# A hybrid decoder trunk on one core: all four FFNs begin with two eight-product pairs, with the token scales between them

## The chip, the cores and the metric

The kernel runs on one core of one Trainium2 chip. Its engines are TensorE (PE, with its weight loads as PEld), VectorE (DVE), ScalarE (ACT), GpSimd (POOL) and SyncE (SP); SP and POOL issue most of the DMAs. The metric is device time in microseconds (us) of one execution; lower is better.

## The reference, cut to what matters

Two layers over 512 tokens of width 1024, all in float32. Each layer has two half-step SwiGLU FFNs (width 2816) around a token mixer (retention in layer 0, forgetting attention in layer 1), and then a gated per-layer embedding ("ple"). So the order is FFN 0, retention, FFN 1, ple 0, FFN 2, attention, FFN 3, ple 1, final norm.

```python
def rmsnorm(x, w):
    y = xf * lax.rsqrt(jnp.mean(xf * xf, axis=-1, keepdims=True) + EPS)
    return (y * w).astype(x.dtype)

def swiglu(x, w_in, w_out):
    g, u = jnp.split(x @ w_in, 2, axis=-1)
    return (jax.nn.silu(g) * u) @ w_out
...
        h = h + 0.5 * swiglu(rmsnorm(h, nw[0]), ffn_w_in[i, 0], ffn_w_out[i, 0])
        hn = rmsnorm(h, nw[1])
        h = h + retention(hn, ...)   # layer 1: forgetting_attention
        h = h + 0.5 * swiglu(rmsnorm(h, nw[2]), ffn_w_in[i, 1], ffn_w_out[i, 1])
        gate = jax.nn.sigmoid(rmsnorm(h, nw[3]) @ ple_w_gate[i])
        h = h + gate * (p[i] @ ple_w_proj[i])
```

## The kernel before, in words

The residual stream `h` lies transposed in SBUF: 8 blocks of 128 features x 512 tokens. Every operand of a product is split into a high and a low fp32r half, and a product is three matmuls (high x high, high x low, low x high). A row norm is not applied to the operands beforehand: only the gain is, and the products are multiplied by the token's scale afterwards. The scale comes in two steps. `Norm.columns` sums the squares over the features with eight small matmuls (L310 in `over_tokens`) and takes the reciprocal root on ScalarE and VectorE (L448 to L452, tile `cols`). `Norm.rows` spreads it over the partitions with four transposes (L443, `spread`) and a ScalarE copy (L437, tile `rows`). The square sum `acc` is split into halves by `halved` (L287, L288, tile `tmp`) when its last block is in.

An FFN's input weights come as 22 `Pair`s, each one gate tile and one up tile of 128 outputs. A pair is taken in one of two ways:

- **Eight products** (`plain`, L507): the plain block products, 96 matmuls of 128x128 by 256 tokens. The pair's two parts `q` and `r` (512 KB each) stand in the plan as ordinary chunks, each cast by ScalarE (L78) and subtracted on VectorE (L79).
- **Seven products** (`one`, `two`, `three`, L476): a Winograd form over 2 x 2 blocks, 84 matmuls. It needs sums of the weight's quarters (`emit_sums`: four additions L140, four casts L78 and four subtractions L79, tiles `sums` and `s`), one quarter negated (tile `a`: L116, L117 and an accumulating DMA on POOL's queue, L118), and of the operand also sums of quarters (`quarters`, L360 to L396). `first` loads `q` and splits it, either on ScalarE and VectorE (`direct`) or, otherwise, through another accumulating DMA on POOL's queue. `two` copies a bank (L525), adds (L526), copies again (L528) and adds (L529); `finish` adds on (L542 to L544) and calls `gated`, which multiplies by `rows`, applies Silu and splits the result (L549 to L554, L287, L288).

`PLAIN` says how many pairs of each FFN take eight products: (2, 0, 2, 2). `CHUNKS` cuts the 22 pairs into three chunks; behind each chunk `out_blocks` multiplies its results by the output weights (L296 to L298, 128x512) and adds them to `h` (L568, L571), in the last chunk with the next norm's `block`.

The order on TensorE is the order of the Python code. The queues of the other engines are laid out by a planner that goes by the order in which instructions are traced, by dependences and by its own estimate of when each is ready; on the chip each queue is then worked off in order. Weights follow a written plan, `W.plan`, in which an eight-product pair stands as the two entries `q` and `r` and a seven-product pair as one `Pair`: `take` makes sure that `LOOKAHEAD` = 2 entries behind the one taken have been emitted, and `emit` calls `emit_sums` after each. `W.open` (called ahead of the stage that precedes the FFN's own code) sets from when an FFN's sums may be emitted; in the kernel before, sums of the two pairs next to be used are allowed at once. There are four raw buffers (`wraw`) and three split buffers (`w`) for weights.

How each FFN begins, in TensorE's order:

- FFN 0: `plain(0)`, `plain(1)`, `one(2)`, columns, `two(2)`, `one(3)`, rows, then `gated(0)`, `gated(1)` on the other engines, `two(3)`.
- FFN 1: `one(0)`, `one(1)`, `two(0)`, `two(1)`, columns, `three(0)`, rows.
- FFN 2 and 3: `plain(0)`, columns, `plain(1)`, `one(2)`, rows, `gated(0)`, `gated(1)`, `two(2)`.

`norms[4].extra` and `norms[6].extra` make the norms ahead of FFN 2 and 3 also split the second half of the even blocks (form `b12`), which the eight products need and the seven don't; FFN 0's norm does this in `Norm.plain`.

Of the kernel before, what the change touches and what calls it, by code (L numbers as in the profile page):

```python
# [13 lines left out]
AF = mybir.ActivationFunctionType  # L14
ALU = mybir.AluOpType
# [13 lines left out]
KEPT = 7  # L29
PLAIN = (2, 0, 2, 2)  # L30
CHUNKS = [((0, 6), (6, 14), (14, 22)) if n else ((0, 8), (8, 16), (16, 22)) for n in PLAIN]
H2 = S // 2
# [3 lines left out]
class Pair:  # L36
# [3 lines left out]
    def __init__(self, ffn, q, r):  # L40
        self.ffn, self.q, self.r, self.direct = ffn, q, r, False
# [13 lines left out]
class Weights:  # L55

    def __init__(self, nc, raw_pool, pool):
        self.nc, self.raw_pool, self.pool = nc, raw_pool, pool  # L60
        self.plan, self.ready, self.used = [], [], 0
        self.low = nc.vector
        self.limit, self.spare = None, []
        self.sum_pool, self.open_ffn, self.pairs_used = None, None, 0

    def emit(self, upto):
# [63 lines left out]
    def emit_sums(self):  # L130

        nc = self.nc
        pairs = [p for p in self.plan[: len(self.ready)] if isinstance(p, Pair) and p.ffn == self.open_ffn]
        for pair in pairs[: self.pairs_used + 2]:
            if hasattr(pair, "s"):
# [19 lines left out]
    def open(self, ffn, pool):  # L155
        self.open_ffn, self.sum_pool, self.pairs_used = ffn, pool, 0
        self.emit_sums()

    def take(self, src):
# [13 lines left out]
def trunk(ctx, tc, a):  # L173
    nc = tc.nc
# [14 lines left out]

    W = Weights(nc, wraw, wpool)  # L190

# [125 lines left out]
    class Norm:  # L317
# [107 lines left out]
        def columns(self):  # L425

            total = over_tokens(self.acc_parts)
            self.c = stat.tile([P, NT], F32, name="cols")
            self.v = stat.tile([P, NT], F32, name="cv")
            t = stat.tile([P, NT], F32, name="ct")  # L430
            mean_eps(self.v, total)
            rsqrt(self.c, self.v, t)

# [12 lines left out]
    def rsqrt(out, v, t):  # L446

        nc.scalar.activation(t, v, AF.Sqrt)  # L448
        nc.vector.reciprocal(out, t)
        nc.vector.tensor_tensor(out=t, in0=out, in1=out, op=ALU.mult)  # L450
        nc.vector.scalar_tensor_tensor(out=t, in0=t, scalar=-0.5, in1=v, op0=ALU.mult, op1=ALU.mult)
        nc.vector.scalar_tensor_tensor(out=out, in0=t, scalar=1.5, in1=out, op0=ALU.add, op1=ALU.mult)  # L452

# [32 lines left out]
    def ffn(i, n, nxt, stack, apool, meanwhile=None):  # L486
# [87 lines left out]

        if PLAIN[i]:
            done = PLAIN[i]
            whole = [plain(m) for m in range(done - 1)]
            if i:
                n.columns()
            whole.append(plain(done - 1))  # L580
            start(done)
            one(done)
            if not i:
                n.columns()
                two(done)
                start(done + 1)
                one(done + 1)
            n.rows()
            for m, (g, u) in enumerate(whole):
                gated(m, g, u, True)  # L590
            two(done + 1 if not i else done)
            begun = done + (1 if i else 2)
        else:
            for m in (0, 1):
                start(m)
                one(m)
            two(0)
            two(1)
            n.columns()
            three(0)  # L600
            n.rows()
            finish(0)
            begun, done = 2, 1
        for c, (k0, k1) in enumerate(chunks):
# [564 lines left out]
    norms = [Norm(nw(i), *where[i]) for i in range(8)] + [Norm(fw)]  # L1169
    norms[4].extra = norms[6].extra = ua  # L1170
    first = W.emit_parts(((0, 1), (1, 2), (2, 4)))
    next(first)
# [134 lines left out]
```

## Time and profile before

| | |
|---|---|
| median of the runs shown | 2255.05 us (2253.7 to 2256.75, 3 runs) |
| the profiled execution's own time | 2254.57 us |
| its span | 2252.8 us |
| TensorE busy | 2158.8 us, 96% of the span |
| VectorE, ScalarE, POOL busy | 1467.5, 1211.5, 436.7 us |
| granted TensorE clock, mean | 0.983 of full |
| HBM traffic | 117 GB/s over the span |

The profile is of one execution. In a timeline row stand start and duration in us, engine, line, operation, tiles (out<-in), shape and count, and in brackets the engine's idle time ahead of it with what ended it. In a window row, busy time of each engine stands with the number of instructions, and PEclk is the share of its full clock that TensorE was granted. Matmuls overlap in TensorE's pipeline, so that one of 256 columns is shown as some 276 ns long while in an unbroken run they start 115 ns apart.

### The profile page before, as it was taken

What the parts mean: (1) busy time and instruction counts of PE and PEld (TensorE: products, weight loads), DVE (VectorE), ACT (ScalarE), POOL (GpSimd) and SP (SyncE); (2) the same over time, 40 slices, a digit from 0 to 9 for tenths busy, and PEclk for the clock granted to TensorE, in tenths of its full rate; (3) what the DMA queues carried; (4) which work ended last, traced back from release to release, by engine and by line L of the source; (5) the groups of instructions that cost most, each with busy time, mean ns of one, the idle gap of its engine ahead of it and who ended that gap; (6) DMA issues with size and microseconds to landing.
All of it is one profiled execution on the core that took longest, in us unless ns stands there. A gap on an engine that the chain in (4) does not pass through costs nothing.

```text
span 2252.8 us, 34423 instructions
## 1 busy us (share of the span) xinstructions
PE 2158.8 (96%) x13501; PEld 1940.0 (86%) x13501; DVE 1467.5 (65%) x2661; ACT 1211.5 (54%) x2050; POOL 436.7 (19%) x326
## 2 busy tenths in 40 slices
PE   7999999999999899999997999999899999999998
PEld 7899997888888698988976999898778798999987
DVE  8686766353442876766758677775764686877764
ACT  7465553333233664554545656464786775554553
POOL 0010003444444010110110001013333200110144
PEclk9999999999999999999998999999999999999999
DMA  5465462222222354654522456463222234655531
GB/s 179 104 164 150 137 159 94 88 90 84 86 84 75 108 144 128 154 137 122 133 97 85 113 150 164 129 166 94 88 81 76 75 105 116 166 146 143 150 103 38
DMA packets 84882, 264.98 MB, mean 118 GB/s; under 512 B 9312, under 2 KB 12896, under 8 KB 84720
## 3 DMA queue, kind: packets, MB, share of 16 engines
q1 hardware_dynamic: 63328, 209.78, 28.2%
q0 software_dynamic: 20160, 51.91, 13.8%
q8 instruction: 106, 1.74, 0.3%
q10 hardware_dynamic: 1232, 1.09, 0.2%
q14 instruction: 56, 0.46, 0.1%
HBM read 260.62 MB, written 2.13 MB: 117 GB/s over the span
## 4 chain that ended last, share of the span: by engine, by line
PE 78%; DVE 8%; ACT 6%; issue 3%; DMA 3%; POOL 1%; SPq 0%; DVEq 0%; ACTq 0%; POOLq 0%
PE bank L476 30%; PE bank L298 13%; PE bank L296 13%; PE bank L297 13%; DMA wraw<-in_ffn_w_in 3%; PE bank L507 2%; PE bank L679 2%; PE bank L680 2%; PE bank L681 2%; DVE w L79 1%; DVE sums L140 1%; ACT p L982 1%; ACT w L78 1%; POOL w L79 1%; ACT p L984 1%
## 5 line engine op out<-in xcount | busy, mean ns | idle before, releaser
L78 ACT CAST w<-wraw 128x1024 fp32r<-128x1024 f32 (+1 forms) x245 | 248.6, 1022 | 456.0 <-PE bank L298 276.0
L298 PE MATMUL bank<-unit_a,w 128*128 128x512 f32 x736 | 287.4, 391 | 4.8 <-DVE w L79 3.1
L296 PE MATMUL bank<-unit_a,w 128*128 128x512 f32 x736 | 288.8, 392 | 2.1 <-ACT w L78 2.1
L78 ACT CAST s<-sums 128x512 fp32r<-128x512 f32 x328 | 197.7, 617 | 166.2 <-DVE sums L140 113.8
L297 PE MATMUL bank<-unit_a,w 128*128 128x512 f32 x736 | 286.9, 390 | 0.2 <-DVE unit_a L288 0.2
L79 DVE TENSOR_TENSOR s<-sums,s 128x512 fp32r<-128x512 f32 x328 | 220.4, 685 | 90.6 <-ACT s L78 90.1
L298 PE MATMUL bank<-unit_d,w 128*128 128x512 f32 (+1 forms) x712 | 270.2, 380 | 6.4 <-DVE w L79 6.4
L296 PE MATMUL bank<-unit_d,w 128*128 128x512 f32 (+1 forms) x712 | 271.2, 381 | 2.8 <-ACT w L78 1.8
L79 POOL TENSOR_TENSOR w<-wraw,w 128x1024 fp32r<-128x1024 f32 x90 | 217.0, 2414 | 287.2 <-ACT w L78 275.3
L297 PE MATMUL bank<-unit_d,w 128*128 128x512 f32 (+1 forms) x712 | 270.2, 379 | 1.8 <-DVE unit_d L288 1.8
L79 DVE TENSOR_TENSOR w<-wraw,w 128x1024 fp32r<-128x1024 f32 (+1 forms) x155 | 179.5, 1164 | 40.2 <-ACT w L78 40.0
L118 POOL DMA_DIRECT2D a<-in_ffn_w_in x82 | 71.8, 876 | 684.9 <-ACT a L117 531.8
L476 PE MATMUL bank<-unit_b,s 128*128 128x256 f32 x904 | 191.3, 278 | 0.0
L476 PE MATMUL bank<-unit_a,s 128*128 128x256 f32 x1314 | 188.4, 281 | 2.0 <-ACT unit_a L360 1.0
L476 PE MATMUL bank<-unit_d,s 128*128 128x256 f32 x1140 | 179.0, 277 | 0.0
L476 PEld LDWEIGHTS bank<-unit_a,s 128*128 128x128 f32 x1314 | 169.8, 192 | 3.0 <-ACT unit_a L360 1.2
L568 DVE SCALAR_TENSOR_TENSOR tmp<-bank,rows 128x512 f32<-128x512 f32 x96 | 66.0, 689 | 162.8 <-PE bank L298 161.5
L298 PEld LDWEIGHTS bank<-unit_a,w 128*128 128x128 f32 x736 | 138.2, 188 | 36.1 <-DVE w L79 5.3
L296 PEld LDWEIGHTS bank<-unit_a,w 128*128 128x128 f32 x736 | 138.3, 188 | 32.8 <-ACT w L78 4.5
L298 PEld LDWEIGHTS bank<-unit_d,w 128*128 128x128 f32 x712 | 136.0, 191 | 32.6 <-DVE w L79 8.3
L297 PEld LDWEIGHTS bank<-unit_a,w 128*128 128x128 f32 x736 | 138.3, 188 | 28.3 <-DVE unit_a L288 0.5
L296 PEld LDWEIGHTS bank<-unit_d,w 128*128 128x128 f32 x712 | 136.3, 191 | 30.2 <-ACT w L78 3.4
(266 smaller groups left out, 4754.4 us busy)
## 6 DMA issues: line engine op xcount, KB each, us to landing
wraw<-in_ffn_w_in SPq DMA_DIRECT2D x174, 512.0 KB, 4.2
wraw<-in_ffn_w_out SPq DMA_DIRECT2D x64, 512.0 KB, 5.1
w<-in_ffn_w_in POOLq DMA_DIRECT2D x58, 512.0 KB, 5.5
a<-in_ffn_w_in POOLq DMA_DIRECT2D x82, 256.0 KB, 6.2
wraw<-in_ffn_w_out SPq DMA_DIRECT2D x32, 384.0 KB, 3.8
wraw<-in_ret_qk SPq DMA_DIRECT2D x16, 512.0 KB, 3.5
wraw<-in_ret_v SPq DMA_DIRECT2D x16, 512.0 KB, 3.6
wraw<-in_ret_g SPq DMA_DIRECT2D x16, 512.0 KB, 3.5
```

Of the source, the lines that this page charges most:

```text
L78: self.nc.scalar.copy(hi, raw)
L79: self.low.tensor_tensor(out=lo, in0=raw, in1=hi.bitcast(F32), op=ALU.subtract)
L118: self.nc.gpsimd.dma_start(out=lo, in_=src, accum_op=ALU.add)
L296: nc.tensor.matmul(out, wh, xh, start=first, stop=False)
L297: nc.tensor.matmul(out, wh, xl, start=False, stop=False)
L298: nc.tensor.matmul(out, wl, xh, start=False, stop=last)
L476: add = lambda w, x, start, stop: nc.tensor.matmul(out, w, x, start=start, stop=stop, skip_group_check=True)
L507: nc.tensor.matmul(o[:, HALVES[t]], x[:, ks], y, start=k == t == q == 0, stop=k == KB - 1 and q == 2, skip_group_check=True,)
L568: nc.vector.scalar_tensor_tensor(out=t1, in0=o, scalar=-0.5, in1=n.r, op0=ALU.mult, op1=ALU.mult)
L679: nc.tensor.matmul(os[t], xh, wh[:, js], start=k == 0, stop=False)
L680: nc.tensor.matmul(os[t], xh, wl[:, js], start=False, stop=False)
L681: nc.tensor.matmul(os[t], xl, wh[:, js], start=False, stop=k == KB - 1)
```

## The change

All four FFNs get `PLAIN` = 2 and the chunks (0, 6), (6, 14), (14, 22). All four begin alike: `plain(0)`, columns, `plain(1)`, rows, `one(2)`, `gated(0)`, `gated(1)`, `two(2)`. The norm ahead of FFN 1 gets `extra = ud`. Opening an FFN no longer allows sums; `W.begin`, called right behind `n.columns()`, allows two pairs ahead, and hands over the scale's ScalarE root and its last VectorE instruction, so that sums which `begin` itself emits are queued behind these (`tc.issue_after`).

```diff
-PLAIN = (2, 0, 2, 2)
-CHUNKS = [((0, 6), (6, 14), (14, 22)) if n else ((0, 8), (8, 16), (16, 22)) for n in PLAIN]
+PLAIN = (2, 2, 2, 2)
+CHUNKS = [((0, 6), (6, 14), (14, 22)) for n in PLAIN]
...
+        self.ahead, self.behind = 0, ()
...
     def emit_sums(self):
+        with ExitStack() as order:
+            for ins in self.behind:
+                order.enter_context(self.tc.issue_after(ins.ins))
+            self.emit_sums_now()
+
+    def emit_sums_now(self):
         nc = self.nc
         pairs = [p for p in self.plan[: len(self.ready)] if isinstance(p, Pair) and p.ffn == self.open_ffn]
-        for pair in pairs[: self.pairs_used + 2]:
+        for pair in pairs[: self.pairs_used + self.ahead]:
...
     def open(self, ffn, pool):
-        self.open_ffn, self.sum_pool, self.pairs_used = ffn, pool, 0
+        self.open_ffn, self.sum_pool, self.pairs_used, self.ahead, self.behind = ffn, pool, 0, 0, ()
+
+    def begin(self, behind):
+        self.ahead, self.behind = 2, behind
         self.emit_sums()
+        self.behind = ()
...
-            rsqrt(self.c, self.v, t)
+            return rsqrt(self.c, self.v, t)
...
-        nc.scalar.activation(t, v, AF.Sqrt)
+        root = nc.scalar.activation(t, v, AF.Sqrt)
...
-        nc.vector.scalar_tensor_tensor(out=out, in0=t, scalar=1.5, in1=out, op0=ALU.add, op1=ALU.mult)
+        last = nc.vector.scalar_tensor_tensor(out=out, in0=t, scalar=1.5, in1=out, op0=ALU.add, op1=ALU.mult)
+        return root, last
...
-        if PLAIN[i]:
-            done = PLAIN[i]
-            whole = [plain(m) for m in range(done - 1)]
-            if i:
-                n.columns()
-            whole.append(plain(done - 1))
-            start(done)
-            one(done)
-            if not i:
-                n.columns()
-                two(done)
-                start(done + 1)
-                one(done + 1)
-            n.rows()
-            for m, (g, u) in enumerate(whole):
-                gated(m, g, u, True)
-            two(done + 1 if not i else done)
-            begun = done + (1 if i else 2)
-        else:
-            for m in (0, 1):
-                start(m)
-                one(m)
-            two(0)
-            two(1)
-            n.columns()
-            three(0)
-            n.rows()
-            finish(0)
-            begun, done = 2, 1
+        done = PLAIN[i]
+        whole = [plain(m) for m in range(done - 1)]
+        W.begin(n.columns())
+        whole.append(plain(done - 1))
+        n.rows()
+        start(done)
+        one(done)
+        for m, (g, u) in enumerate(whole):
+            gated(m, g, u, True)
+        two(done)
+        begun = done + 1
...
     norms[4].extra = norms[6].extra = ua
+    norms[2].extra = ud
```

More of the change, by code (lines that the diff above doesn't have):

```diff
@@ L55, with __init__ @@
 class Weights:
-    def __init__(self, nc, raw_pool, pool):
-        self.nc, self.raw_pool, self.pool = nc, raw_pool, pool
+    def __init__(self, tc, raw_pool, pool):
+        self.tc, self.nc, self.raw_pool, self.pool = tc, tc.nc, raw_pool, pool
         self.plan, self.ready, self.used = [], [], 0
-        self.low = nc.vector
+        self.low = self.nc.vector
         self.limit, self.spare = None, []
         self.sum_pool, self.open_ffn, self.pairs_used = None, None, 0
+        self.ahead, self.behind = 0, ()
     def emit(self, upto):
@@ L188, in trunk @@
     dram = ctx.enter_context(tc.tile_pool(name="dram", bufs=1, space=bass.MemoryType.DRAM))
-    W = Weights(nc, wraw, wpool)
+    W = Weights(tc, wraw, wpool)
     def unit(pool):
```

## The prediction, made before the changed kernel was built or run

> **What bounds the kernel now.** I read the page first, then TensorE stage by stage, then its waits, then the timeline around each FFN's start.
>
> ```profile
> span 2252.8 us, 34423 instructions
> PE 2158.8 (96%) x13501; PEld 1940.0 (86%) x13501; DVE 1467.5 (65%) x2661; ACT 1211.5 (54%) x2050; POOL 436.7 (19%) x326
> ```
>
> TensorE sets the time: 96% busy. But its busy share hides slow stretches, so the next view cuts the FFNs' input products (L507 eight-product pairs, L476 seven-product pairs) into windows. Columns: stretch, length, busy time of each engine, granted clock, DMA.
>
> ```profile
> core 0: us, PE busy (x) PEld busy (x) DVE busy (x) ACT busy (x) POOL busy (x), PEclk, DMA share, GB/s
> 5.59:33.32 27.73, 25.50 (x194) 24.14 (x192) 26.75 (x54) 22.82 (x42) 1.92 (x2) 1.00 0.69 220
> 33.32:94.18 60.86, 49.25 (x387) 47.87 (x385) 45.83 (x89) 39.72 (x68) 5.23 (x6) 0.92 0.49 130
> ...
> 779.99:875.09 95.10, 85.46 (x715) 84.38 (x715) 73.27 (x138) 65.93 (x113) 12.21 (x14) 0.96 0.65 159
> 920.37:1005.72 85.35, 80.79 (x674) 80.39 (x672) 63.22 (x112) 54.55 (x95) 11.37 (x13) 0.96 0.66 164
> 1051.02:1104.94 53.92, 53.92 (x470) 53.91 (x468) 40.85 (x72) 34.62 (x60) 6.11 (x7) 1.00 0.58 144
> ...
> 1240.04:1285.44 45.40, 43.63 (x379) 43.43 (x377) 35.24 (x61) 33.10 (x56) 5.24 (x6) 1.00 0.58 140
> 1827.52:1852.39 24.87, 24.18 (x201) 23.97 (x200) 21.69 (x41) 14.60 (x25) 1.76 (x2) 1.00 0.52 148
> 1852.39:1899.46 47.07, 45.30 (x378) 45.10 (x377) 35.33 (x61) 33.49 (x56) 5.23 (x6) 0.96 0.56 135
> 1933.62:2011.05 77.43, 77.43 (x674) 77.43 (x672) 63.97 (x115) 56.05 (x97) 11.37 (x13) 1.00 0.73 180
> 2056.36:2129.63 73.27, 73.27 (x638) 73.27 (x636) 55.83 (x99) 49.37 (x86) 9.61 (x11) 1.00 0.66 165
> ```
>
> The last four rows are FFN 3: two eight-product pairs (24.87), the rest of chunk 0 (47.07), chunks 1 and 2. At full pace 672 products take 77.43, 0.1152 each. FFN 1, which begins without eight-product pairs, is the next three rows above FFN 2's 45.40: 708, 672 and 468 products in 95.10 + 85.35 + 53.92 = 234.4, where 1848 x 0.1152 = 212.9: 21.5 lost. FFN 0 is the first two rows: its 372 products of chunk 0 take 60.86 where FFN 2 needs 45.40.
>
> ```profile
> PE bank L476 <- ACT tmp L528: 11.1, 7, 3.2
> PE bank L443 <- DVE cols L452: 10.0, 2, 6.8
> ...
> PE bank L476 <- ACT unit_a L368: 4.5, 1, 4.5
> ...
> PE bank L476 <- DMA w<-in_ffn_w_in: 2.8, 1, 2.8
> ```
>
> These waits (total, times, longest) are those starts: the token scales (L452) hold TensorE twice, 6.8 in FFN 0 and 3.2 in FFN 1; L368 is FFN 1's first operand.
>
> ```profile
> 22.32 0.69 DVE L288 TENSOR_TENSOR tmp<-acc,tmp 128x512 fp32r<-128x512 f32 x1
> ...
> 43.06 1.29 DVE L140 TENSOR_TENSOR sums<-wraw 128x512 f32<-128x512 f32 x2
> ...
> 50.07 0.15 DVE L452 SCALAR_TENSOR_TENSOR cols<-ct,cols 128x4 f32<-128x4 f32 x1
> 50.37 1.09 PE L443 MATMUL bank<-ident,cols 128*128 128x128 f32 x4 [6.82 <-DVE cols L452]
> ```
>
> In FFN 0 the scales' last step ends at 50.2, behind sums (L140) of pairs that TensorE doesn't need yet.
>
> **Part by part.**
>
> *FFN 1, two eight-product pairs and chunks 6, 8, 8.* Products: 2 x 96 - 2 x 84 = 24 more, and each of the 192 at the pace of this row:
>
> ```profile
> 1827.68 11.51 PE bank L507 x96
> ```
>
> 0.120 each, so 192 x 0.120 + 1680 x 0.1152 = 216.5 against 212.9: +3.6 at full pace, on the path. The output products are as many, only divided otherwise: 0. Other engines, for pairs 0 and 1:
>
> ```profile
> L79 DVE TENSOR_TENSOR s<-sums,s 128x512 fp32r<-128x512 f32 x328 | 220.4, 685 | 90.6 <-ACT s L78 90.1
> L78 ACT CAST s<-sums 128x512 fp32r<-128x512 f32 x328 | 197.7, 617 | 166.2 <-DVE sums L140 113.8
> L79 DVE TENSOR_TENSOR w<-wraw,w 128x1024 fp32r<-128x1024 f32 x123 | 149.3, 1219 | 38.9 <-ACT w L78 38.8
> ```
>
> Gone from VectorE are eight additions and eight subtractions (16 x 0.685 = 11.0) and two conversions (2 x 1.22); four wide conversions come (4 x 1.22 = 4.9), and four half-width splits of `extra`, each under 0.69. VectorE has at least 5.8 less; ScalarE loses eight casts (4.9), gains two wide ones and the four splits. On POOL two accumulating DMAs fall away. SP keeps four 512 KB loads. The forms: `extra` takes four `ud` units, free when the last retention product that reads them is done, before block 7's splits.
>
> What FFN 1 will then cost I take from FFN 3, which has that form already, follows the same output helper, and shows the stalls left over: 24.87 + 47.07 + 77.43 + 73.27 = 222.6. Gain 234.4 - 222.6 = 11.8. Unknown is FFN 1's own start wait: between 0 more than FFN 3 and the 4.46 of the row below. Less is queued on VectorE now, so I take 1. **-10.8**.
>
> ```profile
> 784.45 1.18 PE L476 MATMUL bank<-unit_a,w 128*128 128x256 f32 x2 [4.46 <-ACT unit_a L368]
> ```
>
> *FFN 0: scales between the pairs.* The column sums need both halves of the squares, ready at 23.0 (L288 above), while plain pair 0 ends at 20.45. TensorE idles 2.6, sums columns to 23.9, then does pair 1 in 11.5: 35.4 instead of 33.32, +2.1. The step issues no DMA, passes nothing on SP's or POOL's queues, and keeps its two table loads on ScalarE. The idle time may cost clock too. Granted clock after pauses of 4.46, 2.8, 3.2 and, in FFN 3, 1.77 (its 47.07 less 45.30 busy):
>
> ```profile
> 780.00:788.50 8.50, 4.03 (x17) 3.74 (x18) 7.70 (x17) 6.66 (x11) 0.87 (x1) 0.62 0.72 191
> 65.70:72.50 6.80, 3.97 (x20) 3.97 (x21) 4.03 (x8) 1.50 (x4) 0.87 (x1) 0.75 0.89 233
> 800.91:806.00 5.09, 1.89 (x17) 1.89 (x17) 3.62 (x11) 3.28 (x7) 0.87 (x1) 1.00 0.93 204
> 1861.37:1867.00 5.63, 3.86 (x21) 3.87 (x22) 3.86 (x8) 4.07 (x7) 0.00 (x0) 0.74 0.24 86
> ```
>
> FFN 2's 1.77 left it at 1.00 (its row above). So of four short pauses two lowered the clock, for 6.80 x 0.25 = 1.7 and 5.63 x 0.26 = 1.5. I count half of 1.6: +0.8, bounds 0 and 1.7. [...]
>
> Then scales and the 372 products as in FFN 2: 45.40. But VectorE is full here:
>
> ```profile
> 20.45:33.32 12.87, 11.51 (x94) 11.31 (x94) 12.81 (x26) 12.39 (x24) 1.92 (x2) 1.00 0.47 116
> 33.32:43.55 10.23, 8.95 (x70) 8.14 (x68) 10.23 (x22) 9.40 (x16) 0.87 (x1) 1.00 0.47 125
> ```
>
> It forms the operands' quarters and the sums of pairs 2 and 3 at once. Ahead of pair 3's sums now come the scales (five of about 0.16) and the two gatings (six of 0.69): 4.9. In exchange the sums of pairs 4 and 5 drop behind, and there is no second pair to be begun early. The backlog costs 0 to 4.9; as VectorE has no slack I take 4.0. Chunk 0 ends at 35.4 + 0.8 + 45.4 + 4.0 = 85.6 instead of 94.18: **-8.6**.
>
> *FFN 2 and 3: scales before the first seven-product pair.*
>
> ```profile
> 1226.68 0.95 PE L310 MATMUL bank<-ones_r,tmp 128*128 128x2 f32 x8
> 1229.71 0.16 DVE L452 SCALAR_TENSOR_TENSOR cols<-ct,cols 128x4 f32<-128x4 f32 x1
> 1242.85 0.60 PE L443 MATMUL bank<-ident,cols 128*128 128x128 f32 x4
> 1250.36 0.37 ACT L528 COPY tmp<-bank 128x256 f32<-128x256 f32 x1 [0.35 <-DVE bank L526]
> 1250.79 0.50 PE L476 MATMUL bank<-unit_b,w 128*128 128x256 f32 x2 [1.77 <-ACT tmp L528]
> ```
>
> The scales are there 13 us before L443, so spreading them 24 products (2.8) earlier makes no wait. Gating starts 2.8 earlier; the pause of 1.77 (FFN 3 has the same, with the clock loss above) is ScalarE getting to L528 late, behind gating. It can go whole or not at all, if ScalarE merely does other work first. I take half, 0.9, in FFNs 1, 2 and 3: **-2.7** (bounds 0 and 3 x 1.77 + 1.5 = 6.8).
>
> *Sums behind the scales.* `take` keeps two plan entries ahead. After `plain(0)` has taken two, four entries are ready, and these are the four plain chunks, no `Pair`. So `begin` finds nothing to order and clears `behind`: the edges are never drawn, price 0. In FFN 0 and 1 sums are traced later than before all the same; in FFN 2 and 3 they stand where they stood.
>
> Sum: -10.8 - 8.6 - 2.7 = -22.1. The profiled execution took 2254.57, 0.5 under the median of 2255.05: 2254.6 - 22.1 = **2232.5**.
>
> **Rivals.**
> 1. *FFN 1's long chunk keeps its stalls.* Its chunk 1 has eight seven-product pairs before and after, and lost 85.35 - 77.43 = 7.9 in mid-course, where the chain went through weights:
>
> ```profile
> 849.52 4.74 DMA wraw<-in_ffn_w_in
> ...
> 855.71 1.05 ACT w L116
> ```
>
> A raw buffer is freed, loaded in 4.7, summed, and only then ScalarE proceeds: a ring. Against it: FFN 3's same chunk stalls nowhere. 2232.5 + 7.9 = 2240.
> 2. *FFN 0's scales stay late.* If ready sums still run first on VectorE, TensorE waits at the transposes again, 6.8 and the clock: 2232.5 + 8.3 = 2241. For it: full VectorE. Against: FFN 2's five scale steps took 3 us from L310.
> 3. *The edges are drawn after all.* Then FFN 2's early sums leave the stretch before its first pair, where TensorE starves. Of the sums tile alone:
>
> ```profile
> 1196.63:1217.00 20.37, 5.46 (x9) 0.71 0.31 91
> ```
>
> 2232.5 - 5.5 = 2227. The code speaks against it.
> 4. *Slower.* The ring of rival 1 sets the pace of every start, FFN 0's too (its 2.8 wait on a DMA), so that the order of scales is beside the point. FFN 1 then keeps its 21.5 and pays 3.6 for the 24 products, FFN 0 pays 2.1 for columns and gains nothing: 2254.6 + 5.7 = 2260. It decides once less than 5.7 of those losses go. Against it: FFN 2 and 3 have the ring and no such losses.
>
> **How the numbers follow.** Forecast (about 2223 to 2238) 0.56; rival 1 0.17; rival 2 0.11; rival 3 0.04; rival 4 0.07; something that leaves the time within 0.2% 0.05 (4.5 us: about what a measurement here can tell from no change). Faster 0.56 + 0.17 + 0.11 + 0.04 = 0.88, same 0.05, slower 0.07. Low end: no backlog, no start wait, all pauses gone: -11.8 - 13.4 - 6.8 = -32, 2222. High end: rivals 1 and 2 together, 2232.5 + 16.2 = 2249.
>
> **What would show it.** FFN 1: 192 L507 products in about 25, then 372 in 45 to 47, then 77.4 and 73.3. FFN 0: a pause near 2.6 before L310, L443 without a wait near 35.5, chunk 0 over at 83 to 88. FFN 2 and 3: L443 before L476, the 1.77 shorter, early sums (x9) where they were. Wrong would be: L476 waiting on L528 in FFN 1's chunk 1, L443 waiting on L452, or a long wait for unit_d or unit_c forms in FFN 1.

## The result and the profile after

The changed kernel took 2240.94 us (median of four runs, 2237.4 to 2245.6), the kernel before 2255.9 on the same chip (2253.7 to 2257.95): ratio 0.9935, 95% interval 0.9914 to 0.9956. It is faster, by 15 us where 22 were forecast; 2240.94 lies inside the range (2222 to 2249) and 8.4 above the predicted 2232.5.

The profiled execution was the longest of the four, 2245.6. The same program on another chip gave 0.9969 (0.9956 to 0.9982), a gain of some 6 us there. Single runs of one kernel lie 6 to 14 us apart (the retention stage alone takes 451.8, 453.4 or 455.0 in different runs of kernels with the same code there), so below I read stretches of TensorE, and compare totals only by their intervals.

The lines of the changed kernel are some 12 higher: eight-product pairs L520 (before L507), seven-product pairs L489 (L476), column sums L322 (L310), transposes of the scales L455 (L443), last step of the scales L464 (L452), the additions of `two` L538, L539, L541, L542 (L525 to L529), gating L562 to L567 (L549 to L554); a weight's cast and subtraction L79, L80 (L78, L79), its additions L148 (L140), ScalarE's write ahead of an accumulating DMA L118 (L117), and that DMA on POOL's queue L119 (L118); `split` of anything else L299, L300 (L287, L288), the operand's quarters L372, L373 (L360, L361). These are the page's first lines after:

```profile
span 2243.8 us, 34408 instructions
PE 2161.2 (96%) x13525; PEld 1942.3 (87%) x13525; DVE 1461.6 (65%) x2645; ACT 1205.9 (54%) x2036; POOL 435.2 (19%) x322
```

VectorE is 5.9 less busy, ScalarE 5.6, and TensorE has the 24 products more: the bookkeeping of the change came out as written. Next the windows after, cut as before: FFN 0's eight-product pairs and the rest of its chunk 0; the same two and chunks 1 and 2 of FFN 1; the rest of chunk 0 of FFN 2 and of FFN 3; chunk 1 of FFN 3.

```profile
core 0: us, PE busy (x) PEld busy (x) DVE busy (x) ACT busy (x) POOL busy (x), PEclk, DMA share, GB/s
5.46:38.50 33.04, 29.12 (x205) 27.65 (x204) 29.77 (x65) 25.11 (x46) 1.92 (x2) 0.90 0.64 200
38.50:92.40 53.90, 46.49 (x376) 45.50 (x374) 44.12 (x78) 37.48 (x65) 5.24 (x6) 0.94 0.55 139
777.59:802.82 25.23, 24.53 (x206) 24.32 (x204) 19.39 (x35) 13.85 (x22) 1.76 (x2) 1.00 0.51 146
802.82:849.96 47.14, 44.87 (x375) 44.67 (x373) 35.46 (x61) 33.15 (x56) 5.24 (x6) 0.96 0.57 135
884.12:962.48 78.36, 77.69 (x673) 77.49 (x672) 61.89 (x112) 54.19 (x94) 11.35 (x13) 1.00 0.70 172
1007.77:1081.04 73.27, 73.27 (x637) 73.27 (x636) 56.24 (x99) 49.65 (x86) 9.63 (x11) 1.00 0.65 163
1228.28:1273.70 45.42, 43.19 (x375) 43.00 (x373) 35.17 (x61) 32.90 (x56) 5.24 (x6) 1.00 0.58 140
1840.58:1887.95 47.37, 44.98 (x376) 44.78 (x373) 35.53 (x61) 33.24 (x56) 5.24 (x6) 0.96 0.56 134
1922.11:2001.17 79.06, 77.78 (x673) 77.57 (x672) 64.45 (x115) 55.30 (x96) 11.41 (x13) 1.00 0.70 177
```

FFN 1 now takes 25.23 + 47.14 + 78.36 + 73.27 = 224.0 instead of 234.4. FFN 0's chunk 0 ends at 92.40 instead of 94.18. FFN 2 and FFN 3 are no shorter, and FFN 3's chunk 1 is 1.6 longer. The waits of TensorE after (total, times, longest) say what stands there now:

```profile
PE bank L489 <- ACT tmp L541: 13.4, 6, 5.5
...
PE bank L322 <- ACT tmp L299: 2.2, 1, 2.2
```

The waits for the scales (10.0 in the view before) and for FFN 1's first operand (4.5) are gone. In their place stands one group that was 11.1 and is 13.4: TensorE ahead of pair 2's second half (`three`) waiting for ScalarE's second bank copy of `two` (four times at pair 2, twice more, for 0.7 and 0.3, in later chunks). FFN 2 and attention together are 0.9 longer.

### The profile page after: what moved, and what is told of

Its sections match the earlier page's. It is cut to its first block, busy times and chain, and to the rows that moved or that the text cites. A ratio compares the mean times of both kernels' runs of the same rounds, so it can differ in the third digit from the quotient of the medians.

```text
span 2243.8 us, 34408 instructions
## 1 busy us (share of the span) xinstructions
PE 2161.2 (96%) x13525; PEld 1942.3 (87%) x13525; DVE 1461.6 (65%) x2645; ACT 1205.9 (54%) x2036; POOL 435.2 (19%) x322
## 3 DMA queue, kind: packets, MB, share of 16 engines
q0 software_dynamic: 19584, 50.34, 13.5%
## 4 chain that ended last, share of the span: by engine, by line
PE 82%; DVE 8%; ACT 5%; issue 2%; DMA 1%; POOL 0%; SPq 0%; DVEq 0%; ACTq 0%; POOLq 0%
PE bank L489 30%; PE bank L310 14%; PE bank L308 14%; PE bank L309 14%; PE bank L520 4%; PE bank L674 2%; PE bank L675 2%; PE bank L676 2%; DVE w L80 1%; DMA wraw<-in_ffn_w_in 1%; DVE s L80 1%; ACT w L79 1%; ACT p L977 1%; DVE sums L148 1%; ACT p L979 1%
## 5 line engine op out<-in xcount | busy, mean ns | idle before, releaser
L79 ACT CAST w<-wraw 128x1024 fp32r<-128x1024 f32 (+1 forms) x249 | 252.9, 1023 | 465.7 <-PE bank L310 270.2
L310 PE MATMUL bank<-unit_a,w 128*128 128x512 f32 x736 | 287.9, 391 | 4.8 <-DVE w L80 3.1
L310 PE MATMUL bank<-unit_d,w 128*128 128x512 f32 (+1 forms) x712 | 269.9, 379 | 6.7 <-DVE w L80 6.7
L80 POOL TENSOR_TENSOR w<-wraw,w 128x1024 fp32r<-128x1024 f32 x90 | 218.4, 2429 | 289.5 <-ACT w L79 275.3
L79 ACT CAST s<-sums 128x512 fp32r<-128x512 f32 x320 | 191.3, 617 | 150.9 <-DVE sums L148 100.5
L80 DVE TENSOR_TENSOR s<-sums,s 128x512 fp32r<-128x512 f32 x320 | 213.6, 685 | 84.0 <-ACT s L79 83.1
L80 DVE TENSOR_TENSOR w<-wraw,w 128x1024 fp32r<-128x1024 f32 (+1 forms) x159 | 184.4, 1165 | 44.1 <-ACT w L79 43.8
L119 POOL DMA_DIRECT2D a<-in_ffn_w_in x80 | 70.3, 879 | 704.2 <-ACT a L118 500.6
L489 PE MATMUL bank<-unit_b,s 128*128 128x256 f32 x880 | 185.5, 278 | 0.0
L489 PE MATMUL bank<-unit_d,s 128*128 128x256 f32 x1140 | 178.7, 276 | 0.0
L489 PE MATMUL bank<-unit_a,s 128*128 128x256 f32 x1260 | 176.1, 277 | 1.9 <-ACT unit_a L372 1.1
L310 PEld LDWEIGHTS bank<-unit_a,w 128*128 128x128 f32 x736 | 138.5, 188 | 36.3 <-DVE w L80 5.3
L308 PEld LDWEIGHTS bank<-unit_a,w 128*128 128x128 f32 x736 | 138.7, 188 | 32.9 <-ACT w L79 4.4
L310 PEld LDWEIGHTS bank<-unit_d,w 128*128 128x128 f32 x712 | 136.0, 191 | 33.0 <-DVE w L80 8.7
L489 PEld LDWEIGHTS bank<-unit_a,s 128*128 128x128 f32 x1260 | 158.8, 188 | 2.7 <-ACT unit_a L372 1.6
```

Of the source, the lines that this page charges most:

```text
L79: self.nc.scalar.copy(hi, raw)
L80: self.low.tensor_tensor(out=lo, in0=raw, in1=hi.bitcast(F32), op=ALU.subtract)
L119: self.nc.gpsimd.dma_start(out=lo, in_=src, accum_op=ALU.add)
L308: nc.tensor.matmul(out, wh, xh, start=first, stop=False)
L310: nc.tensor.matmul(out, wl, xh, start=False, stop=last)
L489: add = lambda w, x, start, stop: nc.tensor.matmul(out, w, x, start=start, stop=stop, skip_group_check=True)
```

## The experiments

Each kernel was timed against the kernel before on one chip. The stretches, from each run's trace in us (in brackets TensorE's idle time inside, the wait for the scales included), are "eight" for the two eight-product pairs and "rest" for the remaining products of chunk 0:

| kernel | ratio (95%) | FFN 0 eight, rest | FFN 1 rest | FFN 2 rest | FFN 3 rest | FFN 3 chunk 1 |
|---|---|---|---|---|---|---|
| before | 1 | 27.7, 60.9 (11.6) | other form | 45.4 (1.8) | 47.1 (1.8) | 77.4 |
| changed | 0.9935 (0.9914-0.9956) | 33.0, 53.9 (7.4) | 47.1 (2.3) | 45.4 (2.2) | 47.4 (2.4) | 79.1 (1.3) |
| e0 no edges | 0.9969 (0.9956-0.9982) | 32.1, 54.2 (7.4) | 47.3 (2.3) | 47.1 (2.2) | 45.6 (2.4) | 81.7 (2.5) |
| e1 FFN 1 only | 0.9970 (0.9956-0.9983) | 29.5, 61.9 (11.7) | 45.4 (1.8) | 45.4 (1.8) | 47.1 (1.8) | 81.5 (2.1) |
| e2 old start of FFN 0 | 0.9971 (0.9961-0.9981) | 27.6, 61.0 (11.7) | 45.5 (2.3) | 45.4 (2.2) | 47.3 (2.4) | 78.1 (0.3) |
| e4 edges drawn | 0.9965 (0.9950-0.9980) | 32.7, 53.9 (7.9) | 47.3 (2.5) | 46.0 (2.8) | 45.7 (2.5) | 81.2 (3.3) |
| e3 rows late | 0.9963 (0.9952-0.9975) | 33.1, 53.7 (7.4) | 47.2 (1.8) | 45.4 (1.8) | 45.4 (1.8) | 80.3 (2.5) |
| e5 gating first | 0.9977 (0.9967-0.9987) | 31.9, 54.7 (8.5) | 48.8 (2.8) | 47.6 (2.7) | 47.9 (2.9) | 82.1 (2.7) |
| e6 columns after pair 1 | 0.9961 (0.9945-0.9976) | 28.8, 55.4 (9.5) | 47.2 (2.3) | 45.5 (2.2) | 45.6 (2.4) | 80.4 (2.6) |
| e7 POOL subtracts | 1.0002 (0.9989-1.0015) | 34.8, 59.3 (11.4) | 47.2 (2.3) | 45.4 (2.2) | 47.4 (2.4) | 79.2 (1.4) |
| e9 eight memsets | 0.9958 (0.9943-0.9973) | 32.9, 53.8 (7.4) | 47.2 (2.3) | 45.4 (2.2) | 45.6 (2.4) | 81.5 (2.2) |
| e10 between the gatings | 0.9933 (0.9918-0.9948) | 33.5, 53.2 (6.6) | 44.7 (1.5) | 44.7 (1.5) | 44.8 (1.6) | 80.4 (2.6) |
| e12 two first | 0.9893 (0.9875-0.9911) | 34.3, 51.2 (5.0) | 43.0 (0) | 43.0 (0) | 43.0 (0) | 79.5 (1.8) |
| e13 and three transfers | 0.9886 (0.9865-0.9906) | 32.0, 51.2 (5.0) | 43.0 (0) | 43.0 (0) | 43.0 (0) | 77.4 (0) |

The first four ask which part of the change carries the gain: no order of sums at all (e0), FFN 1's form alone (e1), all but FFN 0's new start (e2), and the order of sums as its text says (e4).

**e0: the order of the sums taken away.**

```diff
-        self.ahead, self.behind = 2, behind
+        self.ahead, self.behind = 2, ()
```

> The changed kernel with the ordering edges taken out of `begin` (it hands over an empty tuple). Theory A (no pair is ready when `begin` looks, so the edges are never drawn): the same queues, the same time as the changed kernel, 2241 +- 3, and FFN 2's early sums where they were (nine VectorE instructions on tile sums/s before its eight-product pairs are fed). Rival B (the edges do hold sums back): the sums move ahead of the scales and the time rises by 3 or more, to 2244 or above. It is also the anchor on this chip for the other three.

Measured 2245.87 against 2252.19. All five queues of this kernel are, instruction for instruction, those of the changed one: `begin` finds no seven-product pair among the ready entries. That part of the change does nothing, and the run doubles as a second sample of the changed program: 0.9969 here, 0.9935 on the first chip.

**e1: the kernel before with FFN 1's form alone.**

```diff
-PLAIN = (2, 0, 2, 2)
+PLAIN = (2, 2, 2, 2)
...
+    norms[2].extra = ud
```

> The kernel before with only FFN 1 changed: PLAIN (2, 2, 2, 2), chunks 6-8-8 in FFN 1 and extra = ud; FFN 0 keeps its start with two pairs begun early, scales are spread after `one(2)` as before, sums are allowed from `open`. Theory A (FFN 1's form carries the gain, about 10.4 by its product stretches 234.4 -> 224.0): 10 to 11 under before, 2245, FFN 1's four stretches together 222 to 225. Rival B (the gain in FFN 1 comes from the new order of scales and sums, not from the eight-product form): FFN 1's stretches stay above 229 and the kernel is less than 6 under before, 2250 or above.

Measured 2245.12, FFN 1's input products in 24.87 + 45.40 + 77.43 + 73.73 = 221.4. By the totals the whole gain of the change is here; FFN 3's chunk 1, 4.0 longer than before, takes back part of FFN 1's 13.0.

**e2: the changed kernel with FFN 0's old start.**

```diff
+        if i == 0:
+            W.begin(())
+            whole = [plain(m) for m in range(done)]
+            start(done)
+            one(done)
+            n.columns()
+            two(done)
+            start(done + 1)
+            one(done + 1)
+            n.rows()
...
```

> The changed kernel with FFN 0's start as before (plain(0), plain(1), one(2), columns, two(2), one(3), rows, two(3), sums allowed at once); FFN 1 to 3 as changed. Theory A (FFN 0's new order gained only 1.8 because VectorE, full, holds up `two`'s chain in place of the scales): chunk 0 of FFN 0 ends at about 94 again and the time is 1 to 4 above the anchor, 2242 to 2245. Rival B (FFN 0's new order carries a good part of the gain and the profiled execution only had a slow clock): 6 to 9 above the anchor, 2247 to 2250.

Measured 2245.12, e0's time: FFN 0's new start brings nothing that the total shows. In the stretches it brings a little: with the old start chunk 0 ends at 94.15 here, 94.18 in the kernel before and 96.94 in e1; with the new one, and nothing else changed in FFN 0, at 92.40 (changed), 91.46 (e0), 92.00 (e3) and 91.77 (e9). That is 2 to 5 earlier, less than the intervals of the totals resolve.

**e4: the edges drawn.** `begin` no longer clears `behind`; `take_pair` does.

```diff
     def begin(self, behind):
...
-        self.behind = ()
...
     def take_pair(self, pair):
...
+        self.behind = ()
```

> The changed kernel with the edges made real: `behind` is kept until the first seven-product pair is taken, so the sums of pairs 2 and 3 stand behind the root on ScalarE and behind the last scale step on VectorE. Theory A (sums take VectorE from the norm and the quarters when TensorE is starved): FFN 2's eight-product stretch falls from 44.7 to about 39 (up to 5.5 of VectorE work leaves it), FFN 0's quarters end earlier and chunk 0 ends 2 to 4 earlier; 2231 to 2235. Rival B (the sums, now late, are what `one(2)` and `one(3)` wait for): new waits of L489 on DVE s, 2 to 5 in each FFN, no gain: 2240 to 2248.

Measured 2244.06. A window from the start of FFN 2's pairs (20.37 long), sums tile alone (length, VectorE busy, ScalarE busy, granted clock, DMA), the changed kernel and then e4:

```profile
1183.54:1203.91 20.37, 4.52 (x7) 2.42 (x4) 0.74 0.32 91
```

```profile
1184.42:1204.79 20.37, 0.00 (x0) 0.00 (x0) 0.71 0.15 52
```

The sums have left the stretch, but FFN 2's pairs go from 44.7 to 42.5 only, where rival 3 priced 5.5, and the pauses of the four FFNs grow by 0.1 to 0.6 each against e0's. Nothing is left in the total.

The next four ask what holds FFN 0's chunk 0 and the pause before `three(2)`: rows back where they were (e3), gating earlier still (e5), no pause for the columns (e6), a less full VectorE (e7).

**e3: rows late in FFN 1 to 3.**

```diff
-        n.rows()
+        if i == 0:
+            n.rows()
         start(done)
         one(done)
+        if i > 0:
+            n.rows()
```

> The changed kernel with the spreading of the scales (rows) put behind `one(2)` again in FFN 1, 2 and 3; FFN 0 as changed. Theory A (spreading earlier does nothing: the pause before `three(2)` is set by VectorE and ScalarE working through gating, `two` and pair 4's sums, and it grew from 1.77 to 2.2 - 2.4): the pauses are 1.8 each, the time 0 to 2 under the changed kernel. Rival B (spreading earlier did gain, as I predicted, 0.9 each): 2 to 4 above the changed kernel.

Measured 2247.29, and the pause is back at 1.8 in FFN 1 to 3. So spreading the scales earlier lengthened it from 1.77 to 2.2-2.4. The pause was to be halved; the step had the wrong sign. Most of the difference is TensorE's own: with the four transposes (0.36) already done, it reaches `three(2)` 8.55 after pair 2's first product instead of 8.97. ScalarE's second copy is done at almost the same time, in FFN 1 at 10.69 here and at 10.77 in the changed kernel (pair 2 begins at 802.17 and 802.82):

```profile
812.49 0.37 ACT L541 COPY tmp<-bank 128x256 f32<-128x256 f32 x1 [0.35 <-DVE bank L539]
```

```profile
813.23 0.36 ACT L541 COPY tmp<-bank 128x256 f32<-128x256 f32 x1
```

**e5: gating traced ahead of pair 2's start.**

```diff
+        for m, (g, u) in enumerate(whole):
+            gated(m, g, u, True)
         start(done)
         one(done)
-        for m, (g, u) in enumerate(whole):
-            gated(m, g, u, True)
```

> The changed kernel with `gated(0)` and `gated(1)` traced ahead of `start(2)`, in all FFNs; TensorE's order is unchanged. Theory A (FFN 0's pause of 5.5 before `three(2)` is VectorE's order: gated(1) and `two`'s additions stand behind pair 4's sums): gated(1) starts at about 50 instead of 54, the pause falls to 1 to 3, chunk 0 of FFN 0 ends 3 to 6 earlier (with the clock), 2 to 6 under the changed kernel in all. Rival B (VectorE is full whatever the order, so another operand is late instead): the pause moves to another product, chunk 0 ends within 1 of the changed kernel.

Measured 2248.84; the pause is 2.7 to 2.9 in FFN 1 to 3 and 6.6 in FFN 0, where theory A expected 1 to 3. TensorE reaches `three(2)` at 8.55, as in the changed kernel, but the second copy is done at 11.28 in FFN 1 instead of 10.77: gating traced ahead of pair 2 delays the chain of `two` by 0.5.

**e6: FFN 0's columns after pair 1, rows after `one(2)`.**

```diff
-        W.begin(n.columns())
+        if i:
+            W.begin(n.columns())
+        else:
+            W.begin(())
         whole.append(plain(done - 1))
-        n.rows()
+        if i:
+            n.rows()
+        else:
+            n.columns()
         start(done)
         one(done)
+        if i == 0:
+            n.rows()
```

> The changed kernel with FFN 0's columns behind plain(1) and rows behind one(2); no second pair begun early; FFN 1 to 3 as changed. Theory A (the columns' pause of 2.6 and the clock it loses made plain(1) 4 to 5 longer than before, 33.0 against 27.7): FFN 0's first stretch is 28 again; whether chunk 0 ends earlier depends on the scales, which then wait behind VectorE's queue: 372 products in 54 to 57. Time 0 to 4 under the changed kernel. Rival B (the scales come late as in the kernel before: a wait of 5 to 7 before the transposes): 372 products in 60, time equal or up to 2 above.

Measured 2244.97; chunk 0 ends at 89.8. Its windows:

```profile
5.59:34.37 28.78, 26.67 (x201) 24.89 (x200) 27.70 (x56) 23.67 (x43) 1.92 (x2) 1.00 0.67 213
34.37:89.80 55.43, 45.96 (x379) 45.39 (x378) 45.35 (x87) 38.91 (x68) 5.25 (x6) 0.91 0.55 143
```

Without the columns' pause the eight-product pairs run at a clock of 1.00 and take 28.78 instead of 33.04. Of these 4.3 some 0.4 are the transposes, which here stand in the other stretch; the rest is about what the pause and the clock after it cost. But now the transposes wait 9.1 for the scales:

```profile
47.44 1.08 PE L455 MATMUL bank<-ident,cols 128*128 128x128 f32 x4 [9.11 <-DVE cols L464]
```

Even so, the two stretches together take 84.2, against 86.9 in the changed kernel and 88.6 in the kernel before: in FFN 0 the columns' place between the pairs, which the change chose, costs more in these traces than the late scales do. The totals don't resolve it (0.9961 beside e3's 0.9963 on the same chip).

**e7: in FFN 0, POOL instead of VectorE does the subtractions of the weight halves up to pair 3.**

```diff
+        if i == 0:
+            W.low = nc.gpsimd
...
+                if i == 0 and c == 0 and m == done + 1:
+                    W.low = nc.vector
```

> The changed kernel with FFN 0's weight subtractions (line of split's second half) on POOL instead of VectorE until the second seven-product pair is done. Theory A (FFN 0's start is bound by VectorE being full): some 12 subtractions of 0.69 to 1.22 leave VectorE, the quarters and gatings come earlier, the pause of 5.5 falls by 3 or more and chunk 0 ends 3 or more earlier. Rival B (it is the chain through ScalarE, which waits 3.4 in order for a free weight buffer, and POOL's slower subtraction, 2.4 for 128x1024, then makes operands late): chunk 0 ends no earlier, new waits on POOL w or s.

Measured 2253.99: the whole gain is gone. POOL's groups in FFN 0:

```profile
L80 POOL TENSOR_TENSOR s<-sums,s 128x512 fp32r<-128x512 f32 x16 | 22.6, 1462 | 15.0 <-ACT s L79 15.0
L80 POOL TENSOR_TENSOR w<-wraw,w 128x1024 fp32r<-128x1024 f32 x4 | 10.9, 2732 | 20.7 <-ACT w L79 20.7
```

VectorE does these in 685 and 1219 ns, so POOL takes 2.1 to 2.2 times as long here; in the kernel before, its 128x1024 subtraction takes 2414, 1.98 times. Every pause in FFN 0 is longer: 4.8 before the columns, 4.0 before pair 2's second operand, 6.2 before `three(2)`. Rival B came true as far as chunk 0 goes, which ends at 99.67.

But the run can't decide whether FFN 0 lacks VectorE time, because it didn't relieve VectorE: over the two stretches it was busy 76.8 with 121 instructions, against 73.9 with 143 in the changed kernel. Many of its additions of SBUF operands slow down beside POOL's subtractions. This is one group of them up to 95 us, in the changed kernel and in e7:

```profile
L148 DVE TENSOR_TENSOR sums<-sums,wraw 128x512 f32<-128x512 f32 x10 | 6.8, 682 | 0.0
```

```profile
L148 DVE TENSOR_TENSOR sums<-sums,wraw 128x512 f32<-128x512 f32 x10 | 11.5, 1155 | 1.6 <-POOL s L80 1.5
```

In e7, six of the ten overlap a subtraction on POOL and take 1470 ns on average; the other four take 681. What can be tried without that side effect is the order in which VectorE and ScalarE do things, and the last batch tried it.

**e10: the additions of pair 2 between the two gatings.**

```diff
-        for m, (g, u) in enumerate(whole):
-            gated(m, g, u, True)
-        two(done)
+        gated(0, *whole[0], True)
+        two(done)
+        gated(1, *whole[1], True)
```

> The changed kernel with the additions of pair 2 (two) written between the gating of pair 0 and that of pair 1, no longer behind both. Theory A (what holds pair 2's second half is VectorE's order, gating of pair 1 ahead of the additions): the pause before it shrinks from 2.2-2.4 to 1.0-1.6 in FFN 1 to 3 and from 5.5 to 3-4 in FFN 0, which is 4 to 6 us over the four FFNs, clock included: 2239 to 2242. Rival B (ScalarE's copy of the bank is what is late, or the pause moves to pair 3's first product, whose banks are those of pair 0): the sum of idle time in each FFN's chunk 0 stays within 0.3 and the time within 2 us of the changed kernel.

Measured 2238.76. The pause falls to 1.5-1.6 in FFN 1 to 3, as expected, and the clock loss behind it goes too (44.7 is 42.95 plus the pause and 0.2). FFN 0's pause is 4.8, where 3 to 4 were expected.

**e12: the additions of pair 2 ahead of both gatings.**

```diff
-        for m, (g, u) in enumerate(whole):
-            gated(m, g, u, True)
-        two(done)
+        two(done)
+        for m, (g, u) in enumerate(whole):
+            gated(m, g, u, True)
```

> The changed kernel with the additions of pair 2 (two) written ahead of the gating of both eight-product pairs. Theory A (VectorE's order): the pause before pair 2's second half falls under 0.8 in FFN 1 to 3, and FFN 0's from 5.5 to 1-3; 6 to 9 us over the four FFNs, 2236 to 2240. Rival B (banks): pair 3 takes the banks of pair 0, which are free only when its gating is done; the gating is now later, so a wait of TensorE for VectorE's multiplication by the row scales stands before pair 3's first product in place of the other, 1.5 to 3 in each FFN, and the time is 2244 to 2248.

Measured 2231.6, on the same chip as e9's 2245.9, and better than expected. FFN 1's timeline shows why. In the changed kernel:

```profile
804.57 1.28 DVE L562 TENSOR_TENSOR tmp<-bank,rows 128x512 f32<-128x512 f32 x2
...
809.73 0.57 ACT L538 COPY tmp<-bank 128x512 f32<-128x512 f32 x1
...
811.99 0.68 DVE L565 SCALAR_TENSOR_TENSOR tmp<-bank,tmp 128x512 f32<-128x512 f32 x1
812.59 0.42 DVE L539 TENSOR_TENSOR bank<-bank,tmp 128x256 f32<-128x256 f32 x1
...
813.65 0.50 PE L489 MATMUL bank<-unit_b,w 128*128 128x256 f32 x2 [2.27 <-ACT tmp L541]
```

and with the additions first:

```profile
802.33 0.58 ACT L538 COPY tmp<-bank 128x512 f32<-128x512 f32 x1
...
803.79 0.43 DVE L539 TENSOR_TENSOR bank<-bank,tmp 128x256 f32<-128x256 f32 x1
...
805.65 1.28 DVE L562 TENSOR_TENSOR tmp<-bank,rows 128x512 f32<-128x512 f32 x2
```

The first bank copy (L538) stood on ScalarE behind the Silu of both gatings, and the addition (L539) on VectorE behind their multiplications. Put first, they start 3.3 and 4.7 us earlier, counted from pair 2's first product (802.82 and 798.73), and in chunk 0 of FFN 1 to 3 TensorE waits for neither. Rival B's wait of pair 3 for the gated banks did not appear. Windows of e12, FFN 0 in two parts, then the rest of chunk 0 of FFN 1, 2 and 3, and FFN 3's chunk 1:

```profile
5.59:39.88 34.29, 30.27 (x205) 28.48 (x204) 29.84 (x64) 25.02 (x45) 1.92 (x2) 0.90 0.63 195
39.88:91.09 51.21, 46.26 (x375) 45.07 (x374) 43.73 (x78) 37.09 (x65) 5.24 (x6) 0.97 0.56 144
798.73:841.68 42.95, 42.95 (x375) 42.95 (x374) 34.22 (x60) 31.61 (x55) 5.23 (x6) 1.00 0.62 148
1221.93:1264.88 42.95, 42.95 (x376) 42.95 (x374) 34.32 (x61) 31.82 (x56) 5.24 (x6) 1.00 0.63 148
1830.59:1873.54 42.95, 42.95 (x376) 42.95 (x374) 34.48 (x61) 32.11 (x56) 5.24 (x6) 1.00 0.62 148
1907.74:1987.23 79.49, 77.70 (x674) 77.49 (x672) 63.64 (x114) 55.65 (x97) 11.40 (x13) 1.00 0.71 175
```

PE busy equals the window in three rows: 372 products at 0.1155 each, no pause and a clock of 1.00. FFN 0's pause is 2.96 instead of 5.54; what holds that rest was not tried. Later in the FFNs the chain of `two` still holds TensorE now and then, so in FFN 3's chunk 2 for 1.6 (1.5 in e13, not at all in the kernel before). The last row still waits 1.8, as every changed kernel so far does there (0.3 to 3.3).

**e9: eight memsets ahead of POOL's stream.** That last loss is a weight that lands late. This is the changed kernel, ScalarE's write, POOL's issue and the product that waits:

```profile
1942.68 1.05 ACT L118 ACTIVATE w<-wraw 128x1024 fp32r<-128x1024 f32 x1
...
1945.99 0.88 POOL L119 DMA_DIRECT2D w<-in_ffn_w_in  x1 [10.47 <-PE bank L489]
...
1953.54 0.50 PE L489 MATMUL bank<-unit_b,w 128*128 128x256 f32 x2 [1.28 <-DMA w<-in_ffn_w_in]
```

ScalarE is done at 1943.73; other issues follow such a write by some 0.3 us, this one by 2.26, and the transfer then takes 7.5 to 8.8 us to land instead of about 5.5. In the profile before, one transfer is as late (2.25), at 1893 us, at the end of FFN 3's chunk 0, where nothing waits for it.

```diff
+    [nc.gpsimd.memset(spare, 0.0) for _ in range(8)]    # right behind make_identity
```

> The changed kernel with eight small memsets of an unused tile on GpSimd at the very start. Every trace so far has one GpSimd transfer issue that begins 2.25 us after ScalarE released it, at the same place in GpSimd's stream of instructions; before it falls at 1893 us, at the end of FFN 3's chunk 0, where nothing waits for it, and in the changed kernels, whose GpSimd runs four instructions fewer, at 1946 us, ahead of a weight of FFN 3's chunk 1. Theory A (the late issue belongs to the place in the stream): it moves some four transfers earlier, FFN 3's chunk 1 goes from 79 to 81.6 back to 77.4 to 77.8, the wait of 2.49 for that weight is gone, and the time falls by 2 to 3 us. Theory B (the weight is late for where it stands among the transfers): chunk 1 still takes 79 to 81 with a wait for w of 1.3 to 2.7, the time as the changed kernel's.

Measured 2245.9; theory A fell. The late transfer stays the same weight (issued at 1941.32), now eight records later in POOL's stream, and chunk 1 takes 81.5. It is not the place in the instruction stream. But in the traces of the kernel before, the changed one and every experiment up to here the late transfer is, counting POOL's DMAs, the 114th; before it is an `a` tile, after it the `w`, because POOL DMAs ahead of them fell away with FFN 1's first pairs. The profile's DMA rows of after (before: x58 and x82):

```profile
w<-in_ffn_w_in POOLq DMA_DIRECT2D x56, 512.0 KB, 5.5
a<-in_ffn_w_in POOLq DMA_DIRECT2D x80, 256.0 KB, 6.1
```

**e13: e12 with three transfers of one column ahead of the others.**

```diff
+    [nc.gpsimd.dma_start(out=spare[:, x : x + 1], in_=a["small"][:, x : x + 1]) for x in range(3)]
```

> The kernel with the additions of pair 2 ahead of both gatings, and three transfers of one column (128 x 1) into an unused tile issued from GpSimd at the very start. In every trace the transfer that GpSimd issues 2.25 us late is its 114th, whatever instructions stand around it; eight memsets ahead of it did not move it. Theory C (the late one is counted among GpSimd's own transfers): the late one is now what was the 111th, a transfer into an a tile at about 1899 us in FFN 3's output products; the weight at 1931 is issued within 0.3 of ScalarE's write and lands in under 6.5 us instead of 8.7; TensorE's wait of 1.79 for it is gone, FFN 3's chunk 1 takes 77.4 to 77.9 instead of 79.5, and the time is 2228 to 2231, 1 to 3 less than without the transfers, which single runs hardly resolve: the stretch decides. Rival D (the weight at 1931 is late for what surrounds it: this copy of the ScalarE order, or the traffic of the output weights): it stays 2.25 late, chunk 1 takes 79 to 82 and the time 2231 to 2234.

Measured 2228.97 against 2256.17, ratio 0.9886 (0.9865 to 0.9906); beside e12's interval that is no proof in the total, but the stretch is plain. POOL's issues in e13 with ScalarE's writes ahead of them:

```profile
1897.07 0.63 ACT L118 ACTIVATE a<-wraw 128x512 fp32r<-128x512 f32 x1
1899.28 0.86 POOL L119 DMA_DIRECT2D a<-in_ffn_w_in  x1 [33.76 <-ACT s L79]
1914.42 1.05 ACT L118 ACTIVATE w<-wraw 128x1024 fp32r<-128x1024 f32 x1
1916.45 0.86 POOL L119 DMA_DIRECT2D w<-in_ffn_w_in  x1 [16.30 <-ACT s L79]
```

The 114th is now the `a` at 1899.28, issued 1.6 us after its write; the one behind it is issued 1.0 after. The weight of chunk 1 (issued at 1928.32) is 0.3 behind its write, as others are, and FFN 3's chunk 1 is whole:

```profile
1906.74:1984.18 77.44, 77.44 (x674) 77.43 (x672) 63.15 (x114) 54.76 (x95) 11.24 (x13) 1.00 0.72 179
```

Theory C holds for the weight. That the delay split over two transfers was not expected. Nor is it a plain count of transfers: an earlier late one, issued 0.97 after its write, is the 61st in every other trace and the 62nd here, though three were put ahead of it. What is counted stays open. e13 is the best version: faster than before by 1.14% and, by the intervals, than the changed kernel.

## Why the prediction was right or wrong

*FFN 1: right.* Forecast 222.6 and 1 of start wait, 10.8 gained; measured 224.0, 10.4 gained in the profile, and e1 shows that this alone makes the measured difference. The 1 was right by luck: FFN 1 had no start wait of its own (0.70 of idle in its first stretch, as in FFN 3), and a loss of 0.9 in chunk 1, which was not forecast, stands in its place. The four stretches named (25, 45-47, 77.4, 73.3) came as 25.23, 47.14, 78.36, 73.27. Rival 1 (chunk 1 keeps its 7.9 of stalls) did not happen: 0.9 is left, and none in any other kernel.

*FFN 0: the scales' wait went as forecast, the backlog was mis-sized and misplaced; this step failed.* Chunk 0 was to end at 85.6 and ended at 92.40: 1.8 gained, not 8.6. The pause came as worked out (2.25 and 0.40, against 2.6):

```profile
22.27 0.33 PE L322 MATMUL bank<-ones_r,tmp 128*128 128x2 f32 x1 [2.25 <-ACT tmp L299]
23.00 1.65 PE L322 MATMUL bank<-ones_r,tmp 128*128 128x2 f32 x7 [0.40 <-DVE tmp L300]
...
38.15 0.60 PE L455 MATMUL bank<-ident,cols 128*128 128x128 f32 x4
...
41.93 0.39 PE L489 MATMUL bank<-unit_a,s 128*128 128x256 f32 x1 [1.08 <-ACT unit_a L372]
...
55.56 2.93 PE L489 MATMUL bank<-unit_a,w 128*128 128x256 f32 x12 [5.54 <-ACT tmp L541]
```

The transposes (L455) had no wait, so rival 2 is out. But they came at 38.15, not 35.5: the columns ended 0.8 later than worked out, and pair 1 took 13.5 instead of 11.5, a clock loss of 2.0, above the bound of 1.7 and not the 0.8 taken: the granted clock is 0.50 from 22.36 to 29.17. One length of pause has no one price: with the same program and the same pause of 2.2, FFN 2's rest of chunk 0 is 45.4 in the changed kernel's run and 47.1 in e0's, where the clock is 0.50 from 1240.3 to 1243.7.

Behind that, 4.0 were put down for VectorE's backlog, as a delay of the sums. The term was too small and in the wrong place: from the transposes on, chunk 0 took 54.25, 8.9 more than FFN 2's 45.40. Idle time there is 7.4, of which one wait before pair 2's second half is 5.54, and the clock is 0.94. I had taken FFN 2's 45.40 as the pace and looked only at when the *sums* are ready. The chain of `two` was in the profile before as the 1.77, and in FFN 0, with more queued ahead of it on ScalarE and VectorE, the same chain costs three times that. Its addition (L539) stands on VectorE behind the gating of pair 1 (L562):

```profile
53.91 0.68 DVE L562 TENSOR_TENSOR tmp<-bank,rows 128x512 f32<-128x512 f32 x1
54.51 0.42 DVE L539 TENSOR_TENSOR bank<-bank,tmp 128x256 f32<-128x256 f32 x1
```

With the additions first (e12) the wait is 2.96 and the rest of chunk 0 is 51.2. To reorder VectorE helped; whether to relieve it would have, e7 does not tell.

*Rows earlier in FFN 1 to 3: wrong in sign.* Forecast -2.7, measured +0.5 to +0.6 of pause in each. The cause was named in part only: I had ScalarE late at its second copy, behind gating, but in the row that I showed ScalarE itself waits 0.35 for VectorE's addition. With rows earlier, ScalarE's first copy in FFN 1 starts 6.9 after pair 2's first product (809.73 above) instead of e3's 8.9, and VectorE's addition still at 9.8 instead of 9.9: VectorE's order sets the chain's end, which barely moved, while TensorE arrived 0.42 sooner. e5 shows that gating traced earlier delays the chain, e10 and e12 that `two` traced earlier frees it.

*Sums behind the scales: right.* Price 0; e0's queues are the same without the edges, and drawing them (e4) brings nothing in the total, so rival 3's price of 5.5 was wrong as well: 2.2.

*Not foreseen:* FFN 3's chunk 1, 0.7 to 4.6 longer in each kernel but e13. I counted two POOL DMAs that fall away (there were four), and as no more than a saving; they moved the late 114th transfer from a harmless place onto a weight. e1, whose FFN 3 code is that of the kernel before, has it too.

Rival 4 (the ring sets every pace, slower) did not happen. In the profile, the sum from span to span (-9.0): FFN 0 -3.2, retention +1.6 (within its scatter), FFN 1 and the stage behind it -11.6, FFN 2 and attention +0.9, FFN 3 to the end +3.2.

That the time lay inside the range is luck in part. The range reached up to 2249 for rivals 1 and 2, which did not happen; what filled that room, the chain of `two` and the late weight, was not among the rivals.

## What to carry to other kernels

Where a queue that is worked off in order serves both a chain that the busy engine needs next and work that is merely ready, the order in which they are written is worth a run: here moving one line put the short chain first (in FFN 1 the bank copy 3.3 us and the addition 4.7 us earlier) and gave at least as much as the whole change (e12's 0.9893 beside e9's 0.9958 on the same chip; the change itself 0.9935 and 0.9969). A small wait that recurs (1.77 in FFN 2 and again in FFN 3) is worth following to what stands ahead of it on each queue before its neighbours are moved; with the filler traced earlier, as in e5, the wait in FFN 1 grew from 2.3 to 2.8. And four DMAs fewer on POOL's queue moved all later ones up in its count; here that put a late issue (2.26 us instead of 0.3), which had harmed nothing, ahead of a weight that TensorE needs.

## What the runs showed of the hardware that was not expected

- One of POOL's DMA issues begins 2.26 us after its release instead of 0.3: the 114th DMA in all thirteen traces without added transfers, unmoved by eight memsets, moved by three transfers of one column (then 1.6 and 1.0 on two neighbours). An earlier one, the 61st (the 62nd in e13), begins 0.97 after its release. What is counted, no run here shows.
- Pauses of 1.5 to 1.6 left the clock at 1.00 (e10, three times). After pauses of 1.8 to 2.4 it either stayed at 1.00 or was 0.50 for 3.4 us (in the changed kernel 1.00 after the 2.2 in FFN 2, 0.50 after the 2.3 in FFN 1 and the 2.4 in FFN 3), which makes a stretch 1.7 longer (45.4 or 47.1 in FFN 2). Of the longer ones, e4's 2.8 in FFN 2 left it alone (the stretch took 46.0) and e5's 2.8 in FFN 1 halved it for 6.8 us (48.8).
- POOL subtracts 128x512 in 1.46 us and 128x1024 in 2.73 beside a busy VectorE (e7), VectorE in 0.69 and 1.22. VectorE pays too: an addition of 128x512 in SBUF that overlaps one of these takes 1.47 on average instead of 0.68, while its instructions that read a bank keep their times (L539: 0.43 beside one, 0.42 otherwise).
